# Growing sums of weight blocks in SBUF by accumulating DMAs instead of VectorE and GpSimd additions

## The chip, the cores and the metric

The kernel runs on one core of a Trainium2 chip. The metric is the device time of one execution in microseconds. A profiled execution gives, beside its time, a trace of every instruction on the five engines (TensorE, called PE; VectorE, DVE; ScalarE, ACT; GpSimd, POOL; SyncE, SP) and of the DMA queues.

## What is computed

One decoder layer in float32 for 512 tokens of width 1024: attention and a gated spatial unit side by side, an output projection, LayerNorm, then a SwiGLU feed-forward layer of hidden width 2816 and a second LayerNorm. The change lies in the feed-forward layer's first half, the gate and up products:

```python
def swiglu_ffn(x, w_gate, w_up, w_down):
    return (jax.nn.silu(x @ w_gate) * (x @ w_up)) @ w_down

def reference(x, w_in, ..., w_gate, w_up, w_down, ln2_g, ln2_b):
    for l in range(DEPTH):
        mix = hybrid_mixer(x, ...)
        x = layer_norm(DEEPNORM_ALPHA * x + mix, ln1_g[l], ln1_b[l])
        ffn = swiglu_ffn(x, w_gate[l], w_up[l], w_down[l])
        x = layer_norm(DEEPNORM_ALPHA * x + ffn, ln2_g[l], ln2_b[l])
    return x
```

## The kernel before

Every float32 operand of a product is split into a high part (rounded to float32r, copied by ScalarE at line 238) and a low part (the difference, by VectorE or GpSimd at line 239). A product of two such operands is three matmuls: high by high, high by low, low by high.

The gate and up products are done by a scheme with seven products instead of eight for each 2 by 2 arrangement of blocks. Eleven pairs (`Pair`, one for two hidden tiles of 128 columns) each have four weight blocks of 128 x 1024 numbers, 512 KB: a11, a21, a22, a12 (blocks 0, 1, 2, 3 of the pair in `w_gu`). On the side of x, `combine` forms sums of token blocks once, at the end of the first LayerNorm. On the side of the weights, each pair needs the sums S1 = a21 + a22, S2 = S1 + a11, S4 = S2 + a12 and a11 + a21. The seven products of a pair are named p1 (a11), p2 (a12), p3 (S4), p5 (S1), p6 (S2), p7 (a11 + a21) and q4 (a22); q4 is held back into the next pair. Each product (`product`, line 829) is 24 matmuls of 256 columns. Its result lies in a PSUM bank, X, Y or W of the pair, and is taken out by ScalarE (lines 860, 865, 872) and VectorE (lines 844 and 866); lines 897 and 884 on GpSimd finish a hidden tile.

A `Raw` is a block as loaded by SP (line 805), a `Blk` its split form in the buffers "wh" and "wl", of which there are three each. Raw blocks lie in "wr" (two buffers, shared with all other weights), "kl" (two, shared with the rows of LayerNorm) or the two halves of "zg". For the first two pairs (EARLY), a11 and a12 are loaded and split ahead of time into other buffers, with the low part on GpSimd.

The sums S1, S2 and S4 grow in two PSUM banks, "tp" and "pv", half a block in each: `grow` adds on VectorE (line 933) and splits each half from PSUM. LayerNorm's transposes use the same two banks. The sum a11 + a21 is made by GpSimd at line 940, in the tile of a21.

No order is written by hand. `Order` collects all operations with an engine, a cost, what they read and write, and a rank; `plan` simulates the engines by these costs and, on each engine, starts the operation of the lowest rank among those that are ready. Its result is the order of instructions in each engine's queue; at run time each queue goes in that order and waits by semaphores. Its costs are constants: DMA_LAT and the size for a load, MM for three matmuls of 512 columns, MM256 for three of 256 columns.

Of the kernel before, what the change touches and what calls it, by code (L numbers as in the profile page):

```python
# [9 lines left out]
ALU = mybir.AluOpType  # L10
# [19 lines left out]

SAME, CROSS, DMA_LAT, MM, MM256 = 0.15, 0.19, 1.9, 0.643, 0.36
SEQ = ('q1', 'a1', 'q0', 'z', 'q2', 'a0', 'u', 'q3', 's', 'a2', 'a3')
RANK = {"w": 5.0, "rope": 10.0, "att": 4.0, "gelu": -8.0, "z": -2.0, "s": -13.5, "fill": 15.0, "sq": -6.0, "ln": -10.5, "ffn": 8.0, "evac": 3.0}

# [25 lines left out]
class Order:  # L62
# [11 lines left out]
        b.name = f"{b.tag}_{self.uid}"  # L74
        return b

    def op(self, eng, cost, fn, r=(), w=(), base=None, table=None, lock=False):
        o = Op()
        o.eng, o.cost, o.fn, o.table, o.lock = eng, cost, fn, table, lock
        o.lat = DMA_LAT if eng == "SP" else 0.0  # L80
        o.prio = (self.base if base is None else base, len(self.ops))
        o.deps, o.succ, o.bufs = set(), [], []
        for keys, writes in ((r, False), (w, True)):
            for key in keys:
                b, sub = key if isinstance(key, tuple) else (key, None)
                if not b.users:
                    self.bufs.append(b)
                if not b.users or b.users[-1] is not o:
                    b.users.append(o)
                    o.bufs.append(b)  # L90
                for s, x in b.writers.items():
                    if x is not o and (s is None or sub is None or s == sub):
                        o.deps.add(x)
                if writes:
                    for s, xs in b.readers.items():
                        if s is None or sub is None or s == sub:
                            o.deps.update(x for x in xs if x is not o)
                    if sub is None:
                        b.writers, b.readers = {None: o}, {}
                    else:  # L100
                        b.writers[sub], b.readers[sub] = o, []
                else:
                    b.readers.setdefault(sub, []).append(o)
        self.ops.append(o)
        return o
# [80 lines left out]
def build(tc, cp, wp, ap, ps, xt, xtok, w_vqk, w_zu, w_out, w_gu, w_dn, wsp, cst, rows, cols, out):  # L186
    nc = tc.nc
    od = Order()
    V, A, PL, PE = nc.vector, nc.scalar, nc.gpsimd, nc.tensor
# [5 lines left out]
    def dve(n, fn, r, w, per=1.042, **k):  # L195
        od.op("DVE", 0.066 + 0.001 * per * n, fn, r, w, **k)

    def pool(n, fn, r, w, per=2.25, **k):
        od.op("POOL", 0.07 + 0.001 * per * n, fn, r, w, lock=True, **k)

    def dma(kb, fn, r, w, **k):
        od.op("SP", max(0.46, kb / 352.0), fn, r, w, **k)
# [7 lines left out]
    def work(shape, tag, bufs=1, dtype=F32):  # L210
        return od.buf(ap, shape, dtype, tag, bufs)
# [10 lines left out]
    def bank(tag, bufs):  # L222
        return od.buf(ps, [P, S], F32, tag, bufs)
# [27 lines left out]
    class W:  # L251


        def __init__(self, src, tag=None, mid=None, group=None):
            raw = od.buf(wp, [P, WCH], F32, "wr", 2)
            if tag is None:
                h = od.buf(wp, [P, WCH], F32R, "wh", 3)
                l = od.buf(wp, [P, WCH], F32R, "wl", 3)
                self.hi, self.lo = lambda c: h.t[:, c], lambda c: l.t[:, c]
            else:  # L260
                h = l = work([P, 2, WCH], tag, 2 if tag == "qk" else 1, F32R)
                self.hi, self.lo = lambda c: h.t[:, 0, c], lambda c: h.t[:, 1, c]
            self.key = [h, l]
            hk, lk = [(h, "h")] if h is l else [h], [(l, "l")] if h is l else [l]
            every = slice(0, WCH)
            dma(512, lambda: nc.sync.dma_start(raw.t, src), [], [raw], base=RANK["w"])
            if mid is not None:
                mid(raw)
            split(WCH, lambda: raw.t, lambda: self.hi(every), lambda: self.lo(every), [raw], hk, lk, group in WPOOL,
                  near=group in WHI, base=RANK["w"])  # L270
# [513 lines left out]
    PREP, EVAC = RANK["w"], RANK["evac"]  # L784
# [5 lines left out]
    HALF = (slice(0, 512), slice(512, 1024))  # L790
# [5 lines left out]
    class Raw:  # L796


        def __init__(self, p, j, slot):
            if slot in ("wr", "kl"):  # L800
                b = od.buf(wp, [P, WCH], F32, "wr", 2) if slot == "wr" else work([P, WCH], "kl", 2)
                self.t, self.key = (lambda c=slice(0, WCH): b.t[:, c]), b
            else:
                self.t, self.key = (lambda c=slice(0, WCH): zgr.t[:, slot, c]), (zgr, slot)
            dma(512, lambda: nc.sync.dma_start(self.t(), w_gu[4 * p + j]), [], [self.key], base=PREP)

    class Blk:

# [17 lines left out]
    def whole(raw, early=None):  # L826
        return Blk(early).fill(raw.t, raw.key, far=early in EPOOL)
# [81 lines left out]
    first = [[Raw(0, 0, "wr"), Raw(0, 3, "wr")], [Raw(1, 0, 0), Raw(1, 3, 1)]]  # L909
    for p in range(EARLY):  # L910
        blks = [whole(r, 2 * p + i) for i, r in enumerate(first[p])]
        pairs[p].p1(blks[0])
        pairs[p].p2(blks[1])
    RING = ("kl", "kl", "wr", "wr", 0, 1)
    held_back = None
    for p, pair in enumerate(pairs):
        if p == 0:
            a11, a12 = first[0]
            a21, a22 = Raw(0, 1, 0), Raw(0, 2, 1)
        else:  # L920
            a11, a21, a22, a12 = (Raw(p, j, RING[(4 * (p - 1) + j) % 6]) for j in range(4))
        if p >= EARLY:
            pair.p1(whole(a11))

        acc = [bank("tp", 1), bank("pv", 1)]
        s1 = Blk()

        def grow(blk, one, two):
            for side in range(2):
                def step(side=side, o=acc[side]):  # L930
                    x = (lambda: o.t) if two is None else (lambda: two.t(HALF[side]))
                    k = [o] if two is None else [two.key]
                    dve(512, lambda: V.tensor_tensor(out=o.t, in0=x(), in1=one.t(HALF[side]), op=ALU.add),
                        [one.key, *k], [o], lock=two is not None, base=PREP)
                    blk.fill(lambda: o.t, o, 512, 512 * side, lock=False)

                step()

        grow(s1, a21, a22)
        pool(1024, lambda a=a11, b=a21: PL.tensor_tensor(out=b.t(), in0=a.t(), in1=b.t(), op=ALU.add),  # L940
             [a11.key, a21.key], [a21.key], base=PREP)
        pair.p5(s1)
        if held_back:
            held_back[0].q4(held_back[1])
        s2 = Blk()
        grow(s2, a11, None)
        pair.p6(s2)
        if p >= EARLY:
            pair.p2(whole(a12))
        s4 = Blk()  # L950
        grow(s4, a12, None)
        pair.p3(s4)
        pair.p7(whole(a21))
        held_back = pair, whole(a22)
    held_back[0].q4(held_back[1])


# [5 lines left out]
    def down_w(f, tag=None):  # L963
        w = W(w_dn[f], tag)
        if f < FT - 4:
            hh, hl = prob(F32R), tmp(F32R)
            parts, keys = (lambda: hh.t, lambda: hl.t), ([hh], [hl])
        else:
            i = 2 * (FT - 1 - f)
            parts, keys = (lambda: last.t[:, i, :], lambda: last.t[:, i + 1, :]), ([(last, i)], [(last, i + 1)])  # L970
        h, hi = hT[f]
        hk, neg = [(h, (hi, t)) for t in range(2)], -1.0 if f % 2 else 1.0
        act(512, lambda: A.activation(parts[0](), h.t[:, hi, :], AF.Copy, scale=neg), hk, keys[0])
        dve(560, lambda: V.scalar_tensor_tensor(out=parts[1](), in0=h.t[:, hi, :], scalar=neg, in1=parts[0]().bitcast(F32),
                                                op0=ALU.mult, op1=ALU.subtract), [*hk, *keys[0]], keys[1], lock=True)
        return w, parts, keys[0] + keys[1]
# [9 lines left out]
    for f in range(FT - TAIL):  # L986
        w = down_w(f)
# [90 lines left out]
```

## Time and profile before

| | us |
|---|---|
| median of three runs | 571.74 |
| lowest, highest of the three | 570.74, 1094.83 |
| the profiled execution | 570.17 |
| its span, first to last instruction | 568.1 |
| gate and up products, main stretch | 228.7 to 442 of the span |

The profile page gives busy time of each engine, and a trace can be asked for windows of time, groups of instructions, the chain of waits that ended last, and DMA issues. Busy time of TensorE overlaps itself, since matmuls are pipelined; a window's busy time, which counts each moment once, and the idle time in front of an instruction say more. The highest of the three runs is nearly twice the others.

### The profile page before, as it was taken

Reading aid. Unit: us, or ns where it says so; the run is one execution under the profiler, and the core shown is the slowest. Engines: PE = TensorE matmul, PEld = TensorE weight load, DVE = VectorE, ACT = ScalarE, POOL = GpSimd, SP = SyncE. Lnnn points to the kernel's source line nnn. Section 1 sums busy time; section 2 is a strip of 40 time slices with the busy share of each in tenths; the row PEclk is TensorE's granted clock in tenths of the full one; section 3 lists DMA queues with packets and bytes.
Section 4 is the critical chain, followed back from the end, with each engine's and each line's share of the span. In section 5 each row is a group of like instructions: output and inputs, shape, how many; then the busy total and the mean of one; then the engine's idle time right before and its main releaser. Section 6 shows DMA issues by size and latency. Waiting matters only on the chain.

```text
span 568.1 us, 8774 instructions
## 1 busy us (share of the span) xinstructions
PE 547.5 (96%) x3360; PEld 488.6 (86%) x3360; DVE 413.2 (73%) x707; ACT 280.9 (49%) x482; POOL 157.0 (28%) x119
## 2 busy tenths in 40 slices
PE   9999999999899968999999999999999999999994
PEld 5888888887688857999999999999999888888883
DVE  5537779879975699998788788888877723334385
ACT  6323796788864347544545544544455422323211
POOL 0026258613205730253333242343322200000011
PEclk9999999999999979899999999999999999999998
DMA  7745514155715201432332333333124332232311
GB/s 260 265 131 153 140 48 129 43 163 182 226 38 194 102 3 72 144 127 103 112 112 76 115 109 109 116 111 112 38 75 149 112 111 94 92 112 74 112 74 74
DMA packets 21225, 65.51 MB, mean 115 GB/s; under 512 B 2880, under 2 KB 3392, under 8 KB 21184
## 3 DMA queue, kind: packets, MB, share of 16 engines
q1 hardware_dynamic: 21184, 64.96, 34.6%
q8 instruction: 26, 0.43, 0.3%
q14 instruction: 15, 0.12, 0.1%
HBM read 58.66 MB, written 2.10 MB: 107 GB/s over the span
## 4 chain that ended last, share of the span: by engine, by line
PE 94%; DVE 2%; ACT 2%; issue 0%; POOL 0%; DVEq 0%
PE pj L838 22%; PE sc L838 17%; PE pj L245 12%; PE pj L247 12%; PE pj L246 12%; PE sc L245 2%; PE sc L247 2%; PE sc L246 2%; PE pv L481 2%; PE tp L464 1%; PE sc L426 1%; PE pv L247 1%; PE pv L245 1%; PE tp L247 1%; PE tp L245 1%; PE tp L246 1%
## 5 line engine op out<-in xcount | busy, mean ns | idle before, releaser
L239 DVE TENSOR_TENSOR wl<-wr,wh 128x1024 fp32r<-128x1024 f32 (+1 forms) x55 | 71.8, 1306 | 60.7 <-ACT wh L238 60.1
L238 ACT ACTIVATE wh<-wr 128x1024 fp32r<-128x1024 f32 (+1 forms) x58 | 57.8, 999 | 84.4 <-PE sc L247 54.0
L838 PE MATMUL pj<-qk,wh 128*128 128x256 f32 x352 | 65.6, 287 | 1.2 <-ACT wh L238 1.2
L838 PE MATMUL sc<-xh,wh 128*128 128x256 f32 x352 | 64.5, 284 | 0.0
L838 PEld LDWEIGHTS pj<-qk,wh 128*128 128x128 f32 x352 | 55.8, 195 | 1.4 <-ACT wh L238 1.4
L838 PEld LDWEIGHTS sc<-xh,wh 128*128 128x128 f32 x352 | 55.1, 193 | 0.0
L275 POOL TENSOR_TENSOR sm<-sm,only 128x1 f32<-128x1 f32 (+1 forms) x20 | 16.4, 825 | 137.8 <-DVE sm L274 137.7
L838 PE MATMUL pj<-V,wh 128*128 128x256 f32 x288 | 52.6, 283 | 0.0
L838 PE MATMUL pj<-qk,wl 128*128 128x256 f32 x176 | 50.7, 288 | 0.4 <-DVE wl L239 0.4
L838 PE MATMUL sc<-xh,wl 128*128 128x256 f32 x176 | 49.8, 283 | 0.0
L245 PE MATMUL pj<-wh,xh 128*128 128x512 f32 x114 | 46.3, 406 | 0.0
L838 PEld LDWEIGHTS pj<-V,wh 128*128 128x128 f32 x288 | 44.9, 192 | 0.0
L246 PE MATMUL pj<-wl,xh 128*128 128x512 f32 x114 | 44.6, 391 | 0.0
L838 PE MATMUL pj<-V,wl 128*128 128x256 f32 x144 | 40.8, 283 | 0.0
L247 PE MATMUL pj<-wh,xl 128*128 128x512 f32 x96 | 37.7, 393 | 0.0
L239 POOL TENSOR_TENSOR wl<-wr,wh 128x1024 fp32r<-128x1024 f32 x7 | 17.2, 2456 | 72.8 <-ACT wh L238 67.9
L838 PEld LDWEIGHTS pj<-qk,wl 128*128 128x128 f32 x176 | 34.3, 195 | 0.8 <-DVE wl L239 0.8
L838 PEld LDWEIGHTS sc<-xh,wl 128*128 128x128 f32 x176 | 33.9, 192 | 0.0
L238 ACT ACTIVATE wh<-tp 128x512 fp32r<-128x512 f32 x33 | 19.7, 596 | 27.9 <-PE sc L838 26.0
L838 PE MATMUL sc<-ug,wh 128*128 128x256 f32 x176 | 32.1, 283 | 0.0
L239 DVE TENSOR_TENSOR wl<-tp,wh 128x512 fp32r<-128x512 f32 x33 | 22.6, 684 | 8.6 <-ACT wh L238 8.6
L245 PE MATMUL pj<-wh,pr 128*128 128x512 f32 x72 | 28.0, 389 | 0.0
(331 smaller groups left out, 1512.1 us busy)
## 6 DMA issues: line engine op xcount, KB each, us to landing
wr<-w_dn SPq DMA_DIRECT2D x22, 512.0 KB, 3.2
zg<-w_gu SPq DMA_DIRECT2D x16, 512.0 KB, 3.4
wr<-w_gu SPq DMA_DIRECT2D x16, 512.0 KB, 3.5
kl<-w_gu SPq DMA_DIRECT2D x14, 512.0 KB, 3.3
wr<-w_vqk SPq DMA_DIRECT2D x8, 512.0 KB, 3.6
wr<-w_zu SPq DMA_DIRECT2D x8, 512.0 KB, 3.3
wr<-w_out SPq DMA_DIRECT2D x8, 512.0 KB, 4.1
wr<-w_vqk SPq DMA_DIRECT2D x8, 256.0 KB, 4.0
```

Source lines behind the costliest of these rows:

```text
L238: act(n, lambda: A.activation(hi(), src(), AF.Copy), rs, ws_hi, **k)
L239: either("P" if far else "D", n, lambda E: E.tensor_tensor(out=lo(), in0=src(), in1=hi().bitcast(F32), op=ALU.subtract), [*rs, *ws_hi], ws_lo,
L245: PE.matmul(o(), lhsT=lh(), rhs=rh(), start=start, stop=False)
L246: PE.matmul(o(), lhsT=lh(), rhs=rl(), start=False, stop=False)
L247: PE.matmul(o(), lhsT=ll(), rhs=rh(), start=False, stop=stop)
L275: od.op("POOL", 0.3 + 0.165 * n, lambda: PL.tensor_tensor(out=o.t, in0=v.t, in1=mhalf.t[:, :n], op=ALU.pow), [v, mhalf], [o], lock=True)
L426: PE.matmul(sc.t[:, :n], lhsT=qs.t[:, e, ts], rhs=ks.t[:, 2 * e + 1, :n], start=False, stop=True)
L464: PE.transpose(tp.t[:, j * P:j * P + P], p.t[:, j * P:j * P + P], ident.t)
L481: PE.matmul(pv.t[:, j * P:], lhsT=vs.t[:, j, h, :], rhs=pt.t[:, j * S:j * S + w], start=j == 0 and i == 0, stop=j == NT - 1 and i == 1)
L838: PE.matmul(o, lhsT=lh(w), rhs=buf.t[:, s + rh, x], start=first and side == k == i == 0, stop=k == 3 and i == 2, skip_group_check=True)
```

## The change

The three sums of a pair now grow in the SBUF tile of a21, and a11 + a21 in the tile of a11. Each addition is one DMA from the block in DRAM, issued by GpSimd with an accumulating operation (`accum_op=ALU.add`), so that a block that two sums need is read from DRAM again. `grow`, the two PSUM banks and GpSimd's addition are gone, and each sum is split whole from SBUF. Each pair has two tiles for this, "zg" for the even pairs and "kl" for the odd ones; a12 and a22 go through "wr". In program order the products of a pair are now p5, p1, q4 of the pair before, p6, p2, p7, p3 (they were p1, p5, q4, p6, p2, p3, p7). Two planner constants for the new DMA are added (cost 1.0, latency 4.0), and MM goes from 0.643 to 0.681, which concerns the plan of the whole kernel.

```diff
--- before.py
+++ after.py
@@ -30,7 +30,8 @@
 
 
 
-SAME, CROSS, DMA_LAT, MM, MM256 = 0.15, 0.19, 1.9, 0.643, 0.36
+SAME, CROSS, DMA_LAT, MM, MM256 = 0.15, 0.19, 1.9, 0.681, 0.36
+GROW, GROW_LAT = 1.0, 4.0
 SEQ = ('q1', 'a1', 'q0', 'z', 'q2', 'a0', 'u', 'q3', 's', 'a2', 'a3')
 RANK = {"w": 5.0, "rope": 10.0, "att": 4.0, "gelu": -8.0, "z": -2.0, "s": -13.5, "fill": 15.0, "sq": -6.0, "ln": -10.5, "ffn": 8.0, "evac": 3.0}
 
@@ -74,10 +75,10 @@
         b.name = f"{b.tag}_{self.uid}"
         return b
 
-    def op(self, eng, cost, fn, r=(), w=(), base=None, table=None, lock=False):
+    def op(self, eng, cost, fn, r=(), w=(), base=None, table=None, lock=False, lat=0.0):
         o = Op()
         o.eng, o.cost, o.fn, o.table, o.lock = eng, cost, fn, table, lock
-        o.lat = DMA_LAT if eng == "SP" else 0.0
+        o.lat = DMA_LAT if eng == "SP" else lat
         o.prio = (self.base if base is None else base, len(self.ops))
         o.deps, o.succ, o.bufs = set(), [], []
         for keys, writes in ((r, False), (w, True)):
@@ -802,7 +803,14 @@
                 self.t, self.key = (lambda c=slice(0, WCH): b.t[:, c]), b
             else:
                 self.t, self.key = (lambda c=slice(0, WCH): zgr.t[:, slot, c]), (zgr, slot)
+            self.p = p
             dma(512, lambda: nc.sync.dma_start(self.t(), w_gu[4 * p + j]), [], [self.key], base=PREP)
+
+        def add(self, j):
+            src = w_gu[4 * self.p + j]
+            od.op("POOL", GROW, lambda: nc.gpsimd.dma_start(self.t(), src, accum_op=ALU.add), [self.key], [self.key],
+                  base=PREP, lat=GROW_LAT)
+            return self
 
     class Blk:
 
@@ -911,47 +919,22 @@
         blks = [whole(r, 2 * p + i) for i, r in enumerate(first[p])]
         pairs[p].p1(blks[0])
         pairs[p].p2(blks[1])
-    RING = ("kl", "kl", "wr", "wr", 0, 1)
     held_back = None
     for p, pair in enumerate(pairs):
-        if p == 0:
-            a11, a12 = first[0]
-            a21, a22 = Raw(0, 1, 0), Raw(0, 2, 1)
-        else:
-            a11, a21, a22, a12 = (Raw(p, j, RING[(4 * (p - 1) + j) % 6]) for j in range(4))
+
+        slots = ("kl", "kl") if p % 2 else (0, 1)
+        a11, chain = Raw(p, 0, slots[0]), Raw(p, 1, slots[1])
+        pair.p5(whole(chain.add(2)))
         if p >= EARLY:
             pair.p1(whole(a11))
-
-        acc = [bank("tp", 1), bank("pv", 1)]
-        s1 = Blk()
-
-        def grow(blk, one, two):
-            for side in range(2):
-                def step(side=side, o=acc[side]):
-                    x = (lambda: o.t) if two is None else (lambda: two.t(HALF[side]))
-                    k = [o] if two is None else [two.key]
-                    dve(512, lambda: V.tensor_tensor(out=o.t, in0=x(), in1=one.t(HALF[side]), op=ALU.add),
-                        [one.key, *k], [o], lock=two is not None, base=PREP)
-                    blk.fill(lambda: o.t, o, 512, 512 * side, lock=False)
-
-                step()
-
-        grow(s1, a21, a22)
-        pool(1024, lambda a=a11, b=a21: PL.tensor_tensor(out=b.t(), in0=a.t(), in1=b.t(), op=ALU.add),
-             [a11.key, a21.key], [a21.key], base=PREP)
-        pair.p5(s1)
         if held_back:
             held_back[0].q4(held_back[1])
-        s2 = Blk()
-        grow(s2, a11, None)
-        pair.p6(s2)
+        pair.p6(whole(chain.add(0)))
         if p >= EARLY:
-            pair.p2(whole(a12))
-        s4 = Blk()
-        grow(s4, a12, None)
-        pair.p3(s4)
-        pair.p7(whole(a21))
-        held_back = pair, whole(a22)
+            pair.p2(whole(Raw(p, 3, "wr")))
+        pair.p7(whole(a11.add(1)))
+        pair.p3(whole(chain.add(3)))
+        held_back = pair, whole(Raw(p, 2, "wr"))
     held_back[0].q4(held_back[1])
 
 
```

## Rows read from the trace of the kernel before

**Rows 1.** Page: busy time of each engine, share of the span, instructions.
```profile
PE 547.5 (96%) x3360; PEld 488.6 (86%) x3360; DVE 413.2 (73%) x707; ACT 280.9 (49%) x482; POOL 157.0 (28%) x119
```

**Rows 2.** Windows by stage: busy us of each engine, PEclk, DMA share, GB/s.
```profile
0.00:196.00 196.00, 192.00 (x934) 156.92 (x935) 143.99 (x341) 121.64 (x233) 74.20 (x55) 1.00 0.47 150
196.00:206.30 10.30, 5.34 (x29) 4.31 (x27) 10.15 (x22) 4.98 (x8) 2.39 (x3) 0.99 0.00 0
206.30:223.40 17.10, 14.81 (x96) 13.56 (x96) 15.39 (x28) 12.22 (x22) 2.33 (x3) 0.81 0.18 63
223.40:228.70 5.30, 3.65 (x27) 3.24 (x27) 5.30 (x11) 2.73 (x5) 0.00 (x0) 1.00 0.00 0
228.70:442.00 213.30, 213.30 (x1757) 212.82 (x1758) 179.23 (x227) 106.03 (x173) 72.64 (x54) 0.99 0.32 107
```

**Rows 3.** Chain that ended last: start, us, engine, tile, line, matmuls; two steps.
```profile
296.66 5.76 PE pj L838 x48
302.42 5.76 PE sc L838 x48
```

**Rows 4.** Timeline of PE: start, us, instruction, idle before it and releaser.
```profile
223.41 0.51 PE L838 MATMUL pj<-V,ptl 128*128 128x256 f32 x2 [2.05 <-ACT cs L860]
...
227.80 0.50 PE L838 MATMUL pj<-qk,wh 128*128 128x256 f32 x2 [1.25 <-ACT wh L238]
228.69 0.39 PE L838 MATMUL pj<-qk,wl 128*128 128x256 f32 x1 [0.40 <-DVE wl L239]
```

**Rows 5.** Windows of 2 us around the stage's start; PEclk is the granted clock.
```profile
208.00:210.00 2.00, 1.85 (x7) 1.21 (x6) 1.69 (x5) 1.86 (x5) 0.63 (x1) 0.50 0.03 8
...
230.00:232.00 2.00, 2.00 (x10) 1.77 (x9) 2.00 (x4) 0.64 (x2) 1.71 (x1) 0.50 0.03 8
232.00:234.00 2.00, 2.00 (x14) 2.00 (x14) 1.93 (x4) 1.84 (x4) 0.00 (x0) 0.66 0.47 141
```

**Rows 6.** Timeline of ACT and DVE: whole splits; the first two rows are one.
```profile
313.85 1.06 ACT L238 ACTIVATE wh<-zg 128x1024 fp32r<-128x1024 f32 x1 [1.43 <-PE pj L838]
...
314.94 1.23 DVE L239 TENSOR_TENSOR wl<-zg,wh 128x1024 fp32r<-128x1024 f32 x1 [0.28 <-ACT wh L238]
...
309.32 2.83 DVE L239 TENSOR_TENSOR wl<-kl,wh 128x1024 fp32r<-128x1024 f32 x1
```

**Rows 7.** Groups, 185 to 442: names, shapes, count, busy us, mean ns, idle before.
```profile
L239 DVE TENSOR_TENSOR wl<-wr,wh 128x1024 fp32r<-128x1024 f32 x15 | 24.6, 1638 | 4.9 <-ACT wh L238 4.6
L239 DVE TENSOR_TENSOR wl<-tp,wh 128x512 fp32r<-128x512 f32 x33 | 22.6, 684 | 8.6 <-ACT wh L238 8.6
...
L933 DVE TENSOR_TENSOR tp<-tp,wr 128x512 f32<-128x512 f32 x9 | 6.2, 690 | 0.0
...
L940 POOL TENSOR_TENSOR kl<-kl,kl 128x1024 f32<-128x1024 f32 x4 | 9.6, 2410 | 11.7 <-DVE pv L933 11.7
L884 POOL TENSOR_TENSOR ptl<-pr 128x256 f32<-128x256 f32 x9 | 8.9, 986 | 34.2 <-ACT pr L882 34.2
```

**Rows 8.** Timelines of DVE and ACT: the first sum's first half.
```profile
226.42 0.69 DVE L933 TENSOR_TENSOR tp<-zg 128x512 f32<-128x512 f32 x1
...
227.15 0.60 ACT L238 ACTIVATE wh<-tp 128x512 fp32r<-128x512 f32 x1
```

**Rows 9.** Timeline of SP: the load of pair 0's growing tile.
```profile
188.32 0.33 SPq L805 DMA_DIRECT2D zg<-w_gu  x1
```

**Rows 10.** DMA issues: count, KB each, median us to landing; line 805's landings.
```profile
wr<-w_gu SPq DMA_DIRECT2D x16, 512.0 KB, 3.5
...
rt<-rt SPq DMA_DIRECT2D x32, 64.0 KB, 2.0
qk<-qk SPq DMA_DIRECT2D x8, 256.0 KB, 3.3
...
DMA to landing us min/median/max: 3.1/3.4/6.7
```

**Rows 11.** Window of 10 us in the first stage, matmuls of 512 columns alone.
```profile
20.00:30.00 10.00, 10.00 (x46) 8.25 (x45) 6.97 (x9) 3.34 (x5) 0.00 (x0) 1.00 0.57 199
```

## The prediction, made before the changed kernel ran

> **What bounds the kernel now.** I read the windows by stage first, because a mean over the span hides that its stages have different limits. The page gives TensorE 96% of the span [rows 1], which says little by itself, since busy matmuls are pipelined. The windows say more: from 228.7 to 442 us, the stage that the change rewrites, PE is busy for all 213.3 us and its weight loads for 212.8, while VectorE is busy 179.2 us, ScalarE 106.0 and GpSimd 72.6, and the DMA engines have a share of 0.32 [rows 2]. The chain of waits agrees: it runs through this stage as matmuls alone, 5.76 us for each 48 of them, so 2.88 us for one product of 24 [rows 3], and seven products make a pair: 20.16 us, eleven pairs. The reader is to see that VectorE, though nearly full, sets nothing here. The change removes no matmul. Work taken off VectorE inside 228.7 to 442 is therefore worth nothing.
>
> What is left to win is where PE stands still. Of the 20.6 us of idle PE in the span, 4.0 lie before 196, 5.0 in 196 to 206.3, 2.3 in 206.3 to 223.4, 1.7 in 223.4 to 228.7 [rows 2], and the rest at the very end, which the change doesn't touch. Three of the waits sit at the first products of the stage [rows 4]: 2.05 us for ScalarE's copy at line 860, then 1.25 us for the high part and 0.40 us for the low part of the first sum of blocks. The granted clock is half (1.2 GHz of 2.4) twice: in 208 to 210 and around it, after PE had stood idle for 5 us, and in 230 to 232, with a mean of 0.66 still in 232 to 234, after the idle gaps up to 228.7 [rows 5].
>
> **The change, part by part.**
>
> *Removed from VectorE, ScalarE, GpSimd.* Line 933 runs 66 half additions (14 groups, of which one stands here) at 0.69 us: 45.5 us of VectorE. The 66 half splits on VectorE at 0.68 us, 45 us, become 33 whole ones; an undisturbed whole one is 1.23 us [rows 6], so 40.6 us. Net: 50 of VectorE's 179 us. ScalarE's 66 half copies become 33 of 1.06 us, which changes it by under 5 us. GpSimd loses eleven additions of 2.41 us, 26.5 us [rows 7]. These also disturb VectorE: a whole split takes 2.83 us instead of 1.23 in places [rows 6], and the mean of the 15 that read "wr" is 1.64 [rows 7]. All of it is priced at 0 in the steady stretch, because PE's matmuls cover it; were that cover gone, it would be worth up to 50 us of VectorE.
>
> *Removed at the start of the stage.* The first sum now needs two PSUM banks that LayerNorm's transposes use too, and VectorE's addition at 226.42, the first after the operand work of `combine`; ScalarE's split follows at 227.15 [rows 8], and PE waits for it. After the change the first sum forms in SBUF: the second load of pair 0 is issued at 188.32, as now [rows 9], lands about 3.4 us later [rows 10], and the accumulation needs only that and GpSimd. The whole split can then fall into ScalarE's and VectorE's gaps before 226. So the waits of 1.25 and 0.40 us go: 1.65 us. With PE running on, I take it that the clock isn't halved behind the gaps: 0.50 x 2 + 0.34 x 2 us [rows 5], so 1.7 us more. The wait of 2.05 us at line 860 stays: the copy follows operand splits on ScalarE, which aren't changed. Bounds: 0 (the planner places the split behind `combine` again) and 1.65 + 1.7 + 2.05 = 5.4 us. I take 1.65 + 1.7 = 3.3 us, rounded down, since both waits that go belong to the removed step.
>
> *Added: 44 accumulating DMAs from GpSimd's queue, four a pair.* No row shows one. Plain loads on SP stay at 46; their two pairs of tiles alternate from pair to pair, so a tile is free about 20 us before its pair comes, against 3.4 us to load it, and SP's order costs nothing. A plain 512 KB load lands 3.1 to 6.7 us after issue, median 3.4; 64 KB from SBUF to SBUF take 2.0 and 256 KB 3.3 [rows 10]. From 64 to 512 KB that is 1.4 us for 448 KB. An accumulation moves the block once like a load (3.4 us, the lower bound), or reads source and destination (1024 KB: 5.0 us), or costs three passes (1536 KB: 6.6 us, the upper bound). Issue occupies SP 0.33 us [rows 9]; for GpSimd I bound it by that and by 1.0 us, its mean for a small multiplication of 128x256 (line 884, 0.99 us [rows 7]). X, from the last wait to data, lies in 3.7 to 7.6; I take 5.0 + 0.6 = 5.6 us, the middle pass count, because an addition can't do without its destination.
>
> *What waits behind it.* The sums S1, S2 and S4 of a pair grow in one tile, so each accumulation waits for the split that reads the sum before. Three buffers of "wh" mean that a split starts when the product three before it ends; it lasts 2.3 us from ScalarE's start to VectorE's end [rows 6]. Count from the start of S1's split: done at 2.3; p5 runs 2.88 to 5.76, p1 to 8.64, the held-back q4 to 11.52, then p6 wants S2. S2's data must be there at 11.52 - 2.3 = 9.2, so X up to 6.9, less two semaphore hops: about 6.7. S4 is wanted by p3 at 20.16, data at 17.9; it is there at 2.3 + X + 2.3 + X: X up to 6.6. The other accumulations have more room (S1's tile has a pair's time, a11's sum about 9 us). With X = 5.6 nothing is late. VectorE's evacuations (line 844) and ScalarE's copies stand in order behind a split that waits; GpSimd's lines 897 and 884 stand behind an accumulation that waits for a split, and their results are wanted only in the down projection, so only their buffers press.
>
> *DMA engines.* 0.32 of 213.3 us for some 43.5 loads (107 GB/s by 213.3 us) is 1.57 us a load. 44 accumulations at once that price take the share to 0.64; at twice to 0.97; at three times to 1.29.
>
> A rule weighed here: the Trainium skill, "Collectives: The Full Stack", the section on the bandwidth ceiling, says that an add in the DMA engines needs two source reads and halves the rate of a copy. By it the share would be 0.97, and the sum above stays as it is as long as an accumulation meets no load; no run here shows it yet.
>
> *The planner's constant.* MM goes from 0.643 to 0.681, while a stretch of the first stage shows 46 matmuls of 512 columns in 10 us, 0.65 for three [rows 11]. Nothing runs slower; every order between engines may shift. PE idles 4.0 us before 196 [rows 2], so this is worth -4 to +4 us; I take 0.
>
> **Sum.** The profiled execution took 570.17 us: span 568.1 and 2.07 around it. 570.2 - 3.3 + 0 = 566.9. The median of the runs shown is 571.74, 1.6 above the profiled one, and the lowest 570.74; I set the forecast between the two bases at 567.5.
>
> **The rivals.**
>
> *Late sums (the other side).* If X exceeds 6.6 us, S2 and S4 are each late by X - 6.6 in every pair, over ten to eleven pairs some 21 us per us of X. At X = 7.6 that is +21: 588. An accumulation that meets a plain load on the engines waits up to that load's 1.57 us, X = 5.6 + 1.57 = 7.2: +12.6, so 579. Slower by 2% begins at X = 7.3 (14.7 us, since 3.3 were gained). For it: three passes, a load in the way, GpSimd's in-order queue. Against: two passes with issue are 5.6. By the Trainium skill's two reads, at a share of 0.97, a load would be in the way nearly always, the 579 of this rival. Chance 0.22.
>
> *DMA engines full.* At three times a load's engine time the stage takes 1.29 x 213.3 = 275 us, +62: 632. For it: nothing but the lack of a row. Chance 0.07.
>
> *Nothing gained.* The split of the first sum is planned behind `combine`, or other idle time takes its place: 570 to 572. Chance 0.23.
>
> *More gained.* The 2.05 us, the other halved clock (0.19 x 17.1 = 3.3 us [rows 2]) and the gaps before 196 go as well: 566.9 - 2 - 3.3 - 2 = 559.6. Nothing in the change aims at the 5 us of idle PE ahead of that clock. Chance 0.08.
>
> *Forecast.* 567.5, own range 564 to 570, chance 0.40.
>
> **How the numbers follow.** 2%, 11.4 us, is about what a measurement of this kernel can tell from no change. Faster by more needs under 560.3: half of "more gained", 0.04. Slower by more needs over 583.2: the full engines 0.07 and about two thirds of late sums, 0.15, so 0.22. The rest, 0.74, is within 2%. The range runs from 560 to 588: below it lie 0.04, above it 0.07 and half of late sums, 0.11.
>
> **What would show it.** Right: PE and its weight loads busy without a break from about 229 to the end of the stage, 2.88 us a product; VectorE near 130 us there; no wait of PE for "wh" at 227.8; granted clock whole from 230; DMA share 0.6 to 0.97. Wrong: PE waiting on ScalarE's "wh" with a DMA behind it, twice a pair and by the same amount each time (late sums); a DMA share at 0.95 and more with plain loads landing late (full engines); GpSimd's issues of several us each, which would hold lines 897 and 884. A gap of PE before 196 that isn't in the rows would be the planner's new order and not the accumulations.

## The result and the profile after

The changed kernel takes 612.24 us (median; 611.23 to 616.44), the kernel before 571.39 on the same chip: a ratio of 1.072, 95% interval 1.065 to 1.079. One execution of the kernel before took 1094.83 us, and the ratio leaves it out. The change costs 40.9 us. The forecast was 567.5 with a range up to 588, so it was wrong, and on the side that its first rival described, but beyond that rival's price.

Line numbers move in the changed kernel: the accumulating DMA is line 811, the matmul 846 (838 before), the splits 239 and 240 (238, 239), the evacuation 852 (844), p7's addition on GpSimd 905 (897), the gated product on GpSimd 892 (884).

The profile after is of the slowest of the executions, 616.44 us, so its parts add up to 46.6 us over the profile before and not to 40.9. The page after: busy time of the engines, the DMA queues (q0 is GpSimd's, q1 SP's), and the chain by engine.

```profile
PE 567.5 (92%) x3360; PEld 503.7 (82%) x3360; DVE 368.6 (60%) x608; ACT 280.1 (46%) x449; POOL 179.0 (29%) x152
...
q1 hardware_dynamic: 21184, 64.96, 32.2%
q0 software_dynamic: 6336, 23.07, 21.6%
...
PE 57%; DMA 19%; DVE 7%; issue 6%; ACT 5%; POOL 4%; SPq 1%; DVEq 0%; ACTq 0%; POOLq 0%
```

VectorE lost 44.6 us of work against [rows 1], as meant, and PE, with the same 3360 matmuls, is busy 20 us longer. The windows by stage say where; the third one begins at the first product on a first sum S1 and ends with the last product, which answers to the last of [rows 2].

```profile
0.00:196.00 196.00, 187.78 (x908) 154.02 (x909) 143.12 (x336) 122.56 (x233) 72.11 (x52) 0.99 0.46 145
196.00:232.39 36.39, 29.25 (x175) 25.92 (x173) 33.18 (x55) 20.41 (x34) 15.34 (x13) 0.91 0.57 139
232.39:487.16 254.77, 230.70 (x1753) 225.02 (x1754) 132.67 (x137) 102.75 (x141) 85.55 (x82) 0.93 0.73 168
487.16:614.70 127.54, 119.76 (x529) 98.69 (x527) 59.66 (x83) 34.39 (x44) 6.03 (x6) 0.99 0.28 96
```

The same windows of the kernel before are 196.00, 31.80, 214.23 and 126.07 us long; the third of them:

```profile
227.80:442.03 214.23, 213.83 (x1759) 213.15 (x1760) 180.15 (x229) 106.05 (x174) 72.67 (x54) 0.99 0.32 107
```

So 4.6 us come ahead of the products on sums, 1.5 in the down projection, and **40.5 in the steady stretch**, whose 213.83 busy us of PE were all but its whole length. After, PE stands still for 24.1 us there, and 1,753 matmuls keep it busy 16.9 us longer than 1,759 did: the granted clock fell from 0.99 to 0.93 in the mean. VectorE is at 132.7 instead of 180.2, and no gain from that is seen.

What PE waits for between 225 and 480 us, by the view of waits (total us, times, longest): the splits of S2, for p6. (p7 writes "sc" out of a sum too, but each of these waits stands at p6, behind q4.)

```profile
PE sc L846 <- ACT wh L239: 12.6, 7, 4.1
...
PE sc L846 <- DVE wl L240: 5.9, 8, 0.8
```

And the splits wait for accumulations: ScalarE's high parts 44.5 us for "kl" and 35.8 for "zg", twelve times each. One pair in detail, as the chain of waits goes through it (start, us, piece):

```profile
315.16 2.89 PE sc L846 x24
...
318.15 0.70 DVE rt L852
...
318.92 0.68 POOL pr L905
...
320.14 0.57 POOL kl L811
...
320.75 1.09 POOL pth L892
321.84 7.51 DMA zg<-w_gu
...
329.43 1.06 ACT wh L239
...
330.52 1.24 DVE wl L240
...
331.80 2.90 PE sc L846 x22
```

Read from above: a product ends, VectorE evacuates it, GpSimd adds for p7 (line 905), GpSimd issues the accumulation of the *next* pair's S1 ("kl"), GpSimd multiplies (line 892), and only then goes S2's accumulation ("zg"), which takes 7.51 us to land. GpSimd's own timeline has the three accumulations that leave together, and a fourth by itself:

```profile
318.92 1.28 POOL L905 TENSOR_TENSOR pr<-rt,rt 128x512 f32<-128x512 f32 x1 [6.32 <-DVE rt L852]
320.14 0.88 POOL L811 DMA_DIRECT2D kl<-w_gu  x1
320.75 1.13 POOL L892 TENSOR_TENSOR pth<-pr 128x256 f32<-128x256 f32 x1
321.84 0.87 POOL L811 DMA_DIRECT2D zg<-w_gu  x1
322.45 1.31 POOL L892 TENSOR_TENSOR pth<-pr 128x256 f32<-128x256 f32 x1
323.70 0.87 POOL L811 DMA_DIRECT2D zg<-w_gu  x1
332.05 0.86 POOL L811 DMA_DIRECT2D zg<-w_gu  x1 [7.47 <-DVE wl L240]
...
DMA to landing us min/median/max: 5.2/6.6/10.0
```

By the view of line 811 in 320 to 324 us the three land 6.7, 7.5 and 8.2 us after issue, the fourth, S4's, after 5.9. S1's split ended at 321.28 (VectorE's part ran 2.23 us instead of 1.23 beside line 905), S2's data were there at 329.35: 8.1 us from the last wait to data, where the prediction's count of the pair left 6.7. PE waited 0.98 and 0.75 us at p6:

```profile
330.54 0.51 PE L846 MATMUL sc<-xh,wh 128*128 128x256 f32 x2 [0.98 <-ACT wh L239]
331.80 0.39 PE L846 MATMUL sc<-xh,wl 128*128 128x256 f32 x1 [0.75 <-DVE wl L240]
```

Here S2's accumulation left 0.6 us after S1's split. In the pair before, S1's split ends at 296.48 (295.26 + 1.22), and S2's accumulation leaves 2.4 us later, behind line 905, which itself runs 2.20 us instead of 1.28, another accumulation and line 892:

```profile
295.26 1.22 DVE L240 TENSOR_TENSOR wl<-kl,wh 128x1024 fp32r<-128x1024 f32 x1
...
298.86 1.20 POOL L811 DMA_DIRECT2D kl<-w_gu  x1
```

The two kinds alternate: over the seven pairs from 296 to 442 us, the time from S1's split to S2's data is 6.9 to 10.2 us.

Elsewhere PE's wait is up to 4.1 us, and behind some of the waits the clock falls: in 260 to 266 us, after the longest, the granted clock is 0.50 for the whole window, 1.2 GHz, and 0.62 in the mean of 354 to 363, after waits of 2.81 and 0.75 us. Behind the 0.98 and 0.75 us of the pair above it stayed whole.

```profile
330.00:336.00 6.00, 4.71 (x37) 4.50 (x38) 4.78 (x5) 3.28 (x5) 2.66 (x2) 1.00 0.49 80
354.00:363.00 9.00, 7.26 (x36) 7.05 (x37) 5.42 (x6) 4.76 (x6) 1.59 (x2) 0.62 0.61 154
...
260.00:266.00 6.00, 5.14 (x23) 4.77 (x22) 0.85 (x2) 0.40 (x1) 0.88 (x1) 0.50 0.55 88
```

### The profile page after: what moved, and what is told of

It is laid out like the page before. It is cut to its first block, busy times and chain, and to the rows that moved or that the text cites. A ratio compares the mean times of both kernels' runs of the same rounds, so it can differ in the third digit from the quotient of the medians.

```text
span 614.7 us, 8748 instructions
## 1 busy us (share of the span) xinstructions
PE 567.5 (92%) x3360; PEld 503.7 (82%) x3360; DVE 368.6 (60%) x608; ACT 280.1 (46%) x449; POOL 179.0 (29%) x152
## 3 DMA queue, kind: packets, MB, share of 16 engines
q1 hardware_dynamic: 21184, 64.96, 32.2%
q0 software_dynamic: 6336, 23.07, 21.6%
## 4 chain that ended last, share of the span: by engine, by line
PE 57%; DMA 19%; DVE 7%; issue 6%; ACT 5%; POOL 4%; SPq 1%; DVEq 0%; ACTq 0%; POOLq 0%
PE sc L846 9%; PE pj L246 9%; PE pj L248 9%; PE pj L247 9%; DMA zg<-w_gu 8%; PE pj L846 7%; DMA kl<-w_gu 6%; ACT wh L239 3%; DVE wl L240 3%; DMA wr<-w_vqk 2%; PE sc L248 2%; PE sc L246 2%; PE sc L247 2%; POOL pr L905 1%; PE pv L482 1%
## 5 line engine op out<-in xcount | busy, mean ns | idle before, releaser
L239 ACT ACTIVATE wh<-wr 128x1024 fp32r<-128x1024 f32 (+1 forms) x65 | 65.1, 1003 | 73.1 <-PE sc L248 54.0
L846 PE MATMUL sc<-xh,wh 128*128 128x256 f32 x352 | 76.4, 316 | 14.9 <-ACT wh L239 12.6
L846 PEld LDWEIGHTS sc<-xh,wh 128*128 128x128 f32 x352 | 64.0, 223 | 17.2 <-ACT wh L239 14.0
L240 DVE TENSOR_TENSOR wl<-zg,wh 128x1024 fp32r<-128x1024 f32 x29 | 41.7, 1438 | 52.5 <-ACT wh L239 52.3
L846 PE MATMUL sc<-xh,wl 128*128 128x256 f32 x176 | 56.5, 321 | 5.9 <-DVE wl L240 5.9
L240 DVE TENSOR_TENSOR wl<-kl,wh 128x1024 fp32r<-128x1024 f32 x24 | 33.1, 1378 | 41.9 <-ACT wh L239 41.8
L239 ACT ACTIVATE wh<-zg 128x1024 fp32r<-128x1024 f32 x29 | 30.7, 1059 | 52.0 <-DMA zg<-w_gu 37.2
L239 ACT ACTIVATE wh<-kl 128x1024 fp32r<-128x1024 f32 x24 | 25.3, 1055 | 52.2 <-DMA kl<-w_gu 44.5
L846 PEld LDWEIGHTS sc<-xh,wl 128*128 128x128 f32 x176 | 39.5, 225 | 7.9 <-DVE wl L240 7.9
L905 POOL TENSOR_TENSOR pr<-rt,rt 128x512 f32<-128x512 f32 x11 | 17.8, 1616 | 75.4 <-DVE rt L852 75.4
```

The source lines that it names most:

```text
L239: act(n, lambda: A.activation(hi(), src(), AF.Copy), rs, ws_hi, **k)
L240: either("P" if far else "D", n, lambda E: E.tensor_tensor(out=lo(), in0=src(), in1=hi().bitcast(F32), op=ALU.subtract), [*rs, *ws_hi], ws_lo,
L846: PE.matmul(o, lhsT=lh(w), rhs=buf.t[:, s + rh, x], start=first and side == k == i == 0, stop=k == 3 and i == 2, skip_group_check=True)
L905: pool(512, lambda: PL.tensor_tensor(out=c.t, in0=u3.t, in1=self.b.t, op=ALU.add), [u3, self.b], [(c, 0), (c, 1)], base=EVAC)
```

## The experiments

The theory taken from this profile: S2 is late in every pair. Part A, accumulations in a bunch share the DMA engines. Part B, S2's accumulation stands in GpSimd's in-order queue behind line 905, another accumulation and line 892. The rivals: an accumulation is by itself too slow for the chain; it is the planner's constant; it is the new order of products. Each run stands beside runs of the kernel before on its own chip (571.3 to 571.7 us). "Stretch" is the steady stretch as above, "ahead" the start of its first product, both of the one execution that was profiled. In e10 to e12 one product fewer stands ahead (1,056 or 1,057 matmuls instead of about 1,080), so their stretch holds one product, 2.88 us, more. Where an expectation from e5 on gives a "stage", it counts from the first gate and up product, about 213 us in the changed kernel (273.9 us there), and not from the first product on a sum.

| run | us | ratio to before, 95% | ahead | stretch |
|---|---|---|---|---|
| before | 571.4 | | 227.80 | 214.23 |
| after | 612.24 | 1.065 to 1.079 | 232.39 | 254.77 |
| e1_plain | 583.91 | 1.017 to 1.025 | 234.29 | 218.94 |
| e2_small_s1_a11 | 594.07 | 1.034 to 1.043 | 231.93 | 231.39 |
| e3_p3_held | 594.35 | 1.035 to 1.044 | 233.31 | 230.52 |
| e4_mm643 | 602.62 | 1.050 to 1.055 | 231.69 | 244.20 |
| e5_evac_on_dve | 605.93 | 1.058 to 1.070 | 232.19 | 243.56 |
| e6_evac_on_dve_held_mm643 | 586.15 | 1.024 to 1.031 | 231.45 | 224.91 |
| e7_before_mm681 | 578.88 | 1.010 to 1.017 | 235.54 | 214.86 |
| e8_hybrid | 580.03 | 1.013 to 1.017 | 233.84 | 218.00 |
| e9_dve_and_small | 584.54 | 1.020 to 1.026 | 229.87 | 224.68 |
| e10_hybrid_mm643 | 574.91 | 1.004 to 1.007 | 225.28 | 222.48 |
| e11_queue_order | 656.09 | 1.145 to 1.152 | 226.87 | 306.00 |
| e12_queue_order_pool | 659.82 | 1.152 to 1.158 | 222.57 | 309.69 |

**Plain loads in the accumulations' place.** The same instructions in the same order on every engine, only the sums aren't formed.

```diff
-nc.gpsimd.dma_start(self.t(), src, accum_op=ALU.add)
+nc.gpsimd.dma_start(self.t(), src)
```

> Every accumulating DMA of the changed kernel becomes a plain load of the same block from the same queue, in the same order with the same waits (the sums are left out, each tile holds the last block loaded). Theory A, bunched additions: an accumulation costs the DMA engines 3.0 us against 1.6 for a plain load, and S2's lands late because S1's of the next pair and that of a11 run beside it (7.5 us against 5.3 alone). With plain transfers each lands in about 4 us even in a bunch, S2 is on time, the stage goes back to PE's pace: about 575 us, PE's waits for the high part of S2 (1 to 4 us in most pairs) gone. Theory B, the chain is too long through GpSimd's issue and the waits alone, whatever the transfer costs: 600 us or more. Theory C, the plan's order with another constant for matmuls is what costs: 605 to 612.

583.91. So 28.3 of the 40.9 us, and 35.8 of the 40.5 in the stretch, are there only because the DMA adds; the rest belongs to the order and the constant. The steady stretch, and line 811's own view (min, median and longest issue in ns; landings):

```profile
234.29:453.23 218.94, 213.72 (x1753) 212.42 (x1754) 140.51 (x137) 104.26 (x141) 73.30 (x83) 0.99 0.59 195
...
L811 POOL DMA_DIRECT2D zg<-w_gu x24: 527/593/762, 206.9 to 437.3; - x24
...
DMA to landing us min/median/max: 3.3/4.3/6.1
```

PE is busy 213.72 us, as before, and the pairs are back at 20.16 us (326.35, 346.51, 366.67). A load lands 3.3 us or more after issue, an accumulation of the changed kernel 5.2 or more.

**The bunch thinned out.** The accumulations of S1 and of a11 + a21 cut to 128 of 1024 columns (64 KB); S2's and S4's whole. The next line of the kernel then takes `self.t(c)` and `src[:, c]`; the order of instructions is again the changed kernel's.

```diff
-            src = w_gu[4 * self.p + j]
+            src, c = w_gu[4 * self.p + j], slice(0, 128 if j in (1, 2) else WCH)
```

> The accumulations for S1 and for a11 + a21 move 64 KB instead of 512 KB (so these sums are made on an eighth of their columns only); those for S2 and S4 stay whole; order and waits are those of the changed kernel. Theory A, bunched additions: S2's accumulation has the engines nearly for itself, lands in 5.3 to 5.9 us instead of 6.2 to 9, X is about 6.2 and under the 6.6 from which it is late: 575 to 580 us. Theory B, S2's accumulation alone is too long for its place: PE's waits stay, 600 us or more.

594.07, more than expected: 18.2 us come back, not the 32 to 37 that part A alone would give. GpSimd's timeline says what is left:

```profile
309.35 2.21 POOL L905 TENSOR_TENSOR pr<-rt,rt 128x512 f32<-128x512 f32 x1 [7.69 <-DVE rt L852]
311.50 0.88 POOL L811 DMA_DIRECT2D kl<-w_gu  x1
312.10 1.05 POOL L892 TENSOR_TENSOR pth<-pr 128x256 f32<-128x256 f32 x1
312.79 1.21 POOL L811 DMA_DIRECT2D zg<-w_gu  x1
```

S2's accumulation now lands 5.7 us after issue, but it is issued at 312.79, 2.4 us after S1's split ended at 310.40 (309.19 + 1.21): 905, the small accumulation and 892 stood ahead of it. 2.4 + 5.7 = 8.1 us again, and PE still waits 0.8 us in most pairs for S2's low part. So the queue of part B is there, in most pairs of this run; what it costs is seen in e9 below.

**p3 and its accumulation held into the next pair.** S4's accumulation leaves the place behind S2's.

```diff
-        pair.p3(whole(chain.add(3)))
-        held_back = pair, whole(Raw(p, 2, "wr"))
+        held_back = pair, whole(Raw(p, 2, "wr")), chain
+    # ahead of each q4:
+    held_back[0].p3(whole(held_back[2].add(3)))
```

> All accumulations stay whole; only the program order of the products changes: p3 of a pair, with its accumulation, is held back into the next pair, ahead of q4, so that S2 has one product (2.88 us) more and S4 two. Late sums: S2 is then on time up to X of about 9.5 us, PE's waits in the stage shrink to under 1 us a pair: 572 to 580. DMA engines full: the traffic is the same, the stage stays as long as the engines need, 600 us or more. Theory C: unchanged too, 605 to 615.

594.35, not 572 to 580. The wait moved from S2 to S1: PE now waits at p5, since S1's accumulation leaves 0.5 us ahead of another, at 321.07 and 321.61; S1's lands after 7.7 us, the other after 11.0.

```profile
329.96 0.50 PE L846 MATMUL pj<-qk,wh 128*128 128x256 f32 x2 [0.48 <-ACT wh L239]
331.22 0.38 PE L846 MATMUL pj<-qk,wl 128*128 128x256 f32 x1 [0.76 <-DVE wl L240]
```

**The constant.** MM back to 0.643 in the changed kernel (e4), and 0.681 in the kernel before (e7).

```diff
-SAME, CROSS, DMA_LAT, MM, MM256 = 0.15, 0.19, 1.9, 0.681, 0.36
+SAME, CROSS, DMA_LAT, MM, MM256 = 0.15, 0.19, 1.9, 0.643, 0.36
```

> Only the planner's constant for three matmuls goes back from 0.681 to 0.643. Theories A and B: the gate and up stage stays about 40 us longer than before, and only the gaps ahead of it (PE idle before 196 us: 8.2 us against 4.0) go: 606 to 610 us. Theory C, the constant is the cause: about 570 us.

> The kernel before with nothing but the planner's constant 0.681 in place of 0.643. If the constant was free (priced 0 in the prediction): 570 to 573. If the constant alone makes the 10 us that came back when it was undone in the changed kernel: 578 to 583. If it costs only the time ahead of the gate/up stage: 575 to 577.

e4 gave 602.62, 9.6 us back, which neither of its expectations had; e7 gave 578.88, 7.5 us lost (interval 5.7 to 9.8). No price of 0, then. But they are not the same microseconds. In e7 the steady stretch is 214.86 us, as before, and the loss lies ahead of it: 8.8 us of idle PE before 196 us instead of 4.0 [rows 2], and a wait for the first sum's high part of 4.42 us instead of 1.25 [rows 4]:

```profile
0.00:196.00 196.00, 187.17 (x907) 153.42 (x908) 144.14 (x336) 122.69 (x233) 71.62 (x52) 0.98 0.45 145
...
235.54:450.40 214.86, 214.56 (x1759) 213.87 (x1760) 179.80 (x227) 106.00 (x174) 73.08 (x54) 0.99 0.31 106
...
235.54 0.80 PE L838 MATMUL pj<-qk,wh 128*128 128x256 f32 x2 [4.42 <-ACT wh L238]
```

In e4 the gain lies in the stretch (244.20 instead of 254.77), with the start hardly moved. I read the constant as a reshuffle of all queues, whose worth depends on what else is tight; which queue does it stays open.

**GpSimd's arithmetic moved to VectorE.** Lines 905 and 892 become VectorE instructions (the edit of 905 is shown, that of 892 is alike); VectorE's share allows it. With other costs, the planner also makes another order on VectorE, ScalarE and GpSimd.

```diff
-            pool(512, lambda: PL.tensor_tensor(out=c.t, in0=u3.t, in1=self.b.t, op=ALU.add), [u3, self.b],
+            dve(512, lambda: V.tensor_tensor(out=c.t, in0=u3.t, in1=self.b.t, op=ALU.add), [u3, self.b],
```

> The addition of p7 (L905) and the gated product (L892) go from GpSimd to VectorE; every accumulation stays whole and in the same order. Theory A2 (an accumulation stands in GpSimd's in-order queue behind L905, which waits for VectorE, and L892, which waits for ScalarE; about 2.4 us of lateness a pair, with the halved clock after each wait): stage down from 273.9 to 250 to 258 us, total 588 to 596. Rival (only the sharing of the DMA engines by accumulations in a bunch makes S2 late, the queue is not worth anything by itself): bunches stay, 608 to 613. VectorE gains about 1.7 us of work a pair, which is no bound at 60% busy.

605.93: 6.3 us back, with intervals that overlap a little; less than theory B alone promised and nearer to the rival. GpSimd's timeline and ScalarE's split of S2:

```profile
361.62 0.86 POOL L811 DMA_DIRECT2D kl<-w_gu  x1 [11.67 <-DMA kl<-w_gu]
362.16 1.21 POOL L811 DMA_DIRECT2D zg<-w_gu  x1
364.23 0.86 POOL L811 DMA_DIRECT2D zg<-w_gu  x1 [0.85 <-DVE wl L240]
...
370.31 1.06 ACT L239 ACTIVATE wh<-zg 128x1024 fp32r<-128x1024 f32 x1 [4.86 <-DMA zg<-w_gu]
```

S1's split ends at 361.87 and S2's accumulation leaves at 362.16, 0.3 us later: the queue is gone. But the next pair's S1 left 0.5 us ahead of it, and S2's lands after 8.1 us. 0.3 + 8.1 = 8.4: as late as ever. Take the queue away, and the bunch is tighter.

**Both at once.** e5's edit together with e2's.

> Both causes taken out at once: L905 and L892 on VectorE (as in e5_evac_on_dve) and the accumulations of S1 and of a11+a21 cut to 64 KB (as in e2_small_s1_a11, so their results are left out); S2 and S4 stay whole. If S2's lateness is made of a bunch in the DMA engines and a queue on GpSimd that each alone keeps it late, the accumulations' cost goes nearly whole: 579 to 584, the stage 237 to 241. If the two simply add up (-18 and -6 from 612): 588. If a whole accumulation by itself (5.4 us, then the split) is too slow for the chain: no better than 594.

584.54 (582.82 to 586.20), next to e1's 583.91: most of the accumulations' cost has gone. In the stretch, 30.1 of its 35.8 us are gone (224.68 against 254.77 and e1's 218.94); that the totals meet is also due to a start 4.4 us earlier than e1's. S1's split ends at 328.76, S2's accumulation leaves at 329.05 and lands after 5.6 us, so 5.9 us from the last wait to data, under the 6.7 that the pair allows; p6 of that pair doesn't wait (p5 does, 0.62 us for S1's low part), and the waits for S2's split in the stretch fall from 18.5 us to 3.7. That is little better than the plain sum of the two (588), so I read them as two causes that nearly add, not as one behind the other; the new order that comes with e5's edit is not told apart from the queue. It also settles the rival "too slow by itself": S2's and S4's accumulations are whole here.

**All that helped, together** (e5's and e3's edits and MM = 0.643).

> The edits of the run before, and p3 with its accumulation held back into the next pair, and the planner's constant back at 0.643. If queue and bunch are both causes and the constant is worth 10 us, they add up to 594 - 10 - 8 = 574 to 580. If GpSimd's queue is nothing: 584 to 586. Below 571 only if no accumulation is late any more.

586.15, not 574 to 580: with whole accumulations the gains don't add up, a pair takes about 21 us, and PE waits up to 0.8 us nine times for S1's low part at p5. The granted clock in this stretch is 1.00 all the same.

**Accumulations off the chain only.** S1 and a11 + a21 by accumulating DMA, S2 and S4 by VectorE in PSUM as before, with p3 ahead of p7; then the same with MM = 0.643. (`grow` and its two banks come back too, and are not shown.)

```diff
-        pair.p6(whole(chain.add(0)))
+        s2 = Blk()
+        grow(s2, a11, chain)
+        pair.p6(s2)
-        pair.p3(whole(chain.add(3)))
+        s4 = Blk()
+        grow(s4, a12, None)
+        pair.p3(s4)
```

> S1 and a11+a21 grow by accumulating DMAs (two a pair), S2 and S4 by VectorE in PSUM as in the kernel before, constant 0.681. If accumulations off the chain of sums are free: stage 229 to 235, total 568 to 575. If every accumulation costs by its engine time or its place in GpSimd's queue: two of four a pair, stage about 250, total 588 to 592.

> e8_hybrid with the planner's constant back at 0.643: S1 and a11+a21 by accumulating DMAs, S2 and S4 on VectorE. If these accumulations are free and the constant alone made e8 slower than the kernel before: 570 to 573; with the split of the first sum's wait at the start of the stage gone too, 567 to 570. If the two accumulations a pair cost anything: 575 and more.

580.03 against e7's 578.88, with the same constant: two accumulations a pair cost about 1 us in all, net of what they save and within the intervals, and the pairs are 20.16 us long (316.62, 336.78, 356.94). 574.91 with the old constant: still 0.4 to 0.7% slower than the kernel before. VectorE fell to 161.5 us in e8's stretch, GpSimd lost its 2.41 us additions [rows 7], and nothing was gained. e10's first product on a sum stands 2.5 us earlier, but that is no gain, since one product of 2.88 us now comes behind it instead of ahead; and PE has a wait of 6.51 us ahead of it (4.96 before) and one of 2.55 us behind it. No version here beats the kernel before.

**Another order in GpSimd's queue** (e5's edit, MM = 0.643; S1's and a11's accumulations forced behind S4's, p7 held into the next pair; the planner's latency of an accumulation 6.0 instead of 4.0; then with GpSimd's arithmetic back on GpSimd).

```diff
-        pair.p5(whole(chain.add(2)))
+        pair.p5(whole(chain.add(2, s4)))
-        pair.p7(whole(a11.add(1)))
+        s4 = chain.op
+        held_back = pair, whole(Raw(p, 2, "wr")), a11.add(1, s4)
```

> All four accumulations whole, L905 and L892 on VectorE, constant 0.643, and another order in GpSimd's queue: S2's alone, then S4's, and behind it that of a11+a21 and S1's of the next pair; p7 is held into the next pair behind p3. S2's accumulation then shares the DMA engines with no other. If sharing is what is left of the loss in e6 (586): 572 to 578, stage 234 to 238, landing of S2's accumulation 5.2 to 5.5. If S1's of the next pair is late instead: PE waits at p5 (n1) once a pair and the total is 585 to 600.

> e11_queue_order with L905 and L892 back on GpSimd. If GpSimd's queue matters only because the next accumulations stand in it: the same as e11 within 4 us, since here S2's accumulation is the first that can go. If L905 and L892 stand ahead of S2's accumulation also here: 8 to 16 us more than e11.

656.09 and 659.82, far worse; the two are 3.7 us apart, which is e12's first expectation, but with the loss elsewhere it says little. S2's accumulation did land after 5.0 to 5.2 us in most pairs, and a pair takes 27.2 us all the same. Part of the chain through one:

```profile
400.55 2.88 PE sc L848 x24
403.43 2.17 PE pj L848 x18
...
405.90 1.06 ACT wh L239
...
406.98 1.24 DVE wl L240
...
408.26 4.31 PE pj L848 x22
...
412.59 0.03 DVE pr L854
...
413.20 1.23 DVE wl L240
```

The split at 405.90 is S4's, for p3. On ScalarE it stands behind p2's activation, which waits for p2's end; S4's accumulation had landed only 0.1 us before that end, so it was hardly in time itself. PE waits 1.42 and 0.76 us. Then p1 of the next pair waits 1.68 us for a11's low part, which stands behind p3's evacuation (line 854) on VectorE. So this order has lost the room that p3 and p1 had, and its total says nothing on sharing. Its bunch does: S4's, a11 + a21's and the next S1's accumulations, issued from 400.51 to 401.58, land after 5.0, 7.4 and 9.9 us, one about every 3 us, which is the engine time of one accumulation (3.02 us, below).

So whether whole accumulations could run without loss in a better order was not shown.

## Why the prediction was wrong, step by step

- **What bounds the kernel: right.** Work taken off VectorE in the stretch bought nothing: 39.6 us less in e1, whose pairs are 20.16 us long as before, and 18 us less in e8.
- **X, an accumulation from the last wait to data: right for one alone, wrong for this kernel.** I took 5.6 us. One with only small ones beside it took 5.9 in e9; in the changed kernel, one alone lands 5.2 to 5.9 us after issue. GpSimd is held 0.87 us by an issue (0.59 for a plain load), near the upper bound of 1.0. The threshold of 6.6 to 6.7 us held roughly: with 8.1 us, 1.4 over it, PE waited 0.98 + 0.75.
- **The step that failed is "With X = 5.6 nothing is late".** It counted an accumulation that leaves at once and meets nothing; the rival let it meet one plain load, and named GpSimd's in-order queue without a price. I wrote that lines 897 and 884 stand behind an accumulation that waits, and never turned the sentence round: the accumulation stands behind them, and they wait for VectorE and ScalarE (2.4 us, e2). And I priced "44 accumulations, four a pair" as if they were spread, though p7's, S2's and the next pair's S1's leave within 4 us of one another: three in a bunch land 6.7, 7.5 and 8.2 us after issue.
- **DMA engines.** At 21.6% of 614.7 us for 44, an accumulation costs 3.02 us of engine time; a plain load costs 32.2% for 64.96 MB, 1.60 us for 0.52 MB: a factor of 1.9. The share in the stretch is 0.73, so the engines aren't full on the mean, and the rival of 632 us was rightly thought unlikely. What counted was the stretch of each pair in which three of them overlap. The factor agrees with the rule of the Trainium skill, "Collectives: The Full Stack", the section on the bandwidth ceiling, that an add in the DMA engines needs two source reads and so halves the rate; the prediction named it and then let it change only a chance.
- **The price of lateness: too low.** 21 us per us of X assumed two late sums a pair and a steady clock. Only S2 was late (S4's accumulation goes alone), once a pair and not twice, which by that formula is 10.5 x 1.4 = 15 us at the lateness of the pair shown; p6's waits were 18.5, so that part of the price was near. The stretch lost 40.5: PE's idle time rose by 23.7 us, and 16.9 more came from slower matmuls, at half the clock behind some of the waits. The clock was priced at the start of the stage, where it would be won, and not in the rival, where it was lost.
- **The start of the stage: no gain.** The waits for the first sum went, as predicted; in their place PE waits 1.69 us for ScalarE's and 0.97 us for VectorE's split of the operand "qk" (the same in e1, so not by the adding), then 0.98 and 0.76 at 241. This was the rival "nothing gained" inside the larger loss.
- **The planner's constant: 0 was wrong.** Alone it costs 7.5 us (e7), outside the bound of 4 that I took from PE's idle time ahead of 196 us. The sign that the prediction named for it is there: the changed kernel has 8.2 us of idle PE ahead of 196, as e7 has 8.8, where 4.0 stood.
- **The sum as measured:** constant 7.5 (e7), the new order with plain loads 5.0 (e1 less e7), adding in the DMA 28.3 (after less e1). As differences of neighbouring runs they make 40.8 of 40.9 us by construction, which proves nothing by itself. The second term is a difference between kernels with different orders; what it is made of stays open, and so does how the constant's loss shares out when all edits are in.

## What to carry to other kernels

A chain of dependent transfers is as late as the queue of the engine that issues it and as the transfers that leave with it: count what stands ahead of an issue, and how many become ready at the same event, before you compare one transfer's latency with the slack. Work that moved off an engine which isn't the bound was worth nothing here, so an edit that does only this has nothing to win and can lose. Where the bound is PE, look at the granted clock behind a wait in a loop too: here 23.7 us of waiting brought 16.9 us of slower matmuls with it, though in e6 waits of up to 1.6 us brought none.

## What was not expected of the hardware

- An accumulating DMA of 512 KB into SBUF lands 5.2 us after issue at best and 10.0 at worst in the changed kernel, where a plain load in the same place lands after 3.3 to 6.1 us (e1), and holds GpSimd for 0.87 instead of 0.59 us.
- Beside a GpSimd addition, VectorE's whole split ran 2.23 us instead of 1.23; in e2 the split kept 1.21 us and the addition took 2.21 instead of 1.28. The Trainium skill, "SBUF — State Buffer", section "Who interferes with whom", has it that a VectorE instruction with two SBUF inputs contends with a GpSimd instruction that reads SBUF; the trace agrees, and with line 905 on VectorE (e5) the same split takes 1.22 us.
